# Latent-attention keys projected with features in rows, two heads per 128, and their turned part placed once for all heads

## The chip, the cores and the metric

One core of one Trainium2 chip runs the whole program. The metric is the device time of one execution in microseconds. The engines work side by side, each through its own instructions in an order fixed when the kernel is built: TensorE (PE in the profile; PEld is its weight load), VectorE (DVE), ScalarE (ACT), GpSimd (POOL); SyncE (SP) issues the transfers.

## The reference

A trunk of two layers over 256 positions of width 1024, in float32. In each layer one input projection feeds three causal token mixers (A: differential attention, 4 heads; B: dilated windows, 4 heads; C: latent attention, 8 heads); their gated sum and a gated feed-forward part follow. The change concerns mixer C:

```python
q = (_rms_norm(c_q, q_norm) @ w_uq).reshape(B, S, C_HEADS, C_NOPE_DIM + C_ROPE_DIM)
q_nope, q_pe = q[..., :C_NOPE_DIM], _rope(q[..., C_NOPE_DIM:], pos)
c_kv, k_pe = c_kv_pe[..., :C_KV_LORA], c_kv_pe[..., C_KV_LORA:]
k_pe = _rope(k_pe[:, :, None, :], pos)[:, :, 0]
kv = (_rms_norm(c_kv, kv_norm) @ w_ukv).reshape(B, S, C_HEADS, C_NOPE_DIM + C_V_DIM)
k_nope, v = kv[..., :C_NOPE_DIM], kv[..., C_NOPE_DIM:]
# scores: q_nope . k_nope + q_pe . k_pe, scale, causal softmax, times v
```

A head's key has 64 features of its own (k_nope, from w_ukv) and 32 that are turned by position (k_pe) and are the same for all 8 heads.

## The kernel before, in words

Every product is made of three matmuls: an operand x is split into a high part (ACT copies it, `hi_of`, line 223) and the residue (DVE subtracts, `lo_of`, lines 228 and 230), and high x high, high x low and low x high are summed in PSUM (`mm3`). The weights come in 294 pieces of up to 1024 columns: SP loads a piece, ACT and DVE split it three pieces ahead of its use (`split_piece`, `take`), and there are five buffers of each kind.

`dense` is a generator that goes through a layer's projections piece by piece; `pump(n)` advances it by n pieces, and `run` writes the smaller work between the pumps: the latent rows (`latent_scaled`, `latent_factors`, `latent_transposed`), in layer 0 also the bias tables on POOL (`tables`, lines 338 to 343), and then `attention`, which steps through 4 units of A, 8 of C and 4 of B, with one pump per step. That is the program's order. The order on each engine is made from it by a planner when the kernel is built (`schedule_with_timeline_sim=True`, line 1147): it simulates the engines and puts next on each what it reckons ready.

PSUM has 8 banks: 4 for the projections (`banks`, a ring) and 4 for attention and transposes (`att`). A bank is used again when the reads of its former content are done.

Latent attention before the change. `latent_scaled` copies the latent rows out of PSUM (cks: 256 key and value features and the 32 to be turned; tokens in partitions) and sums their squares. `latent_factors` makes the norm factors rq and rk (epsilon on DVE, the power on POOL, line 372), turns the 32 features on POOL (`rope`, lines 602 to 605, in the tile kpe) and copies them into k_tm for 8 heads (line 684). `latent_transposed` puts the features into partitions, with the norm's gains (line 693). `mla_up` projects: with the latent columns as the loaded operand and 512 weight columns moving it gets keys and values with tokens in partitions, in four banks (lines 573 to 580):

```python
for lhs, ww, s, e in ((h, wh, k == 0, False), (h, wl, False, False), (lo, wh, False, k == 1)):
    for f in range(2):
        self.mm(pu[b][f], lhs, ww[:, f * 512:f * 512 + 512], s, e)
```

The key half is copied with the factor rk into k_tm (line 588), the value half split with it into vc. Scores need features in partitions, so `head_pair`, called two steps ahead for each of four pairs of heads, transposes q_tm and k_tm on PE: two heads by two token blocks, four transposes for the queries and four for the keys (line 719), and splits both. `scores` then multiplies with 96 features in partitions. Behind the up projection comes the value projection of A (`v_proj`), which takes the next two of the four banks.

Of the kernel before, what the change touches and what calls it, by code (L numbers as in the profile page):

```python
# [12 lines left out]
F32 = mybir.dt.float32  # L13
# [7 lines left out]
DEPTH = 2  # L21
# [28 lines left out]
def weight_plan():  # L50
# [11 lines left out]
    for l in range(DEPTH):  # L62
# [3 lines left out]
        block("mla_w_ukv", l, 2, 0, 1024)  # L66
# [117 lines left out]
class Build:  # L184
# [104 lines left out]
    def setup(self):  # L289
# [29 lines left out]
        self.k_tm = cp.tile([128, 2, 8, 96], F32, name="k_tm")  # L319
# [4 lines left out]
        self.kpe = cp.tile([128, 2, 32], F32, name="kpe")  # L324
# [223 lines left out]
    def mla_up(self):  # L548
# [24 lines left out]
        pu = [[self.banks.get() for _ in range(2)] for _ in range(2)]  # L573
        for k in range(2):
            (wh, wl), = self.take()
            for b in range(2):
                h, lo = (t[:, k * 256 + b * 128:k * 256 + b * 128 + 128] for t in self.ck)
                for lhs, ww, s, e in ((h, wh, k == 0, False), (h, wl, False, False), (lo, wh, False, k == 1)):
                    for f in range(2):
                        self.mm(pu[b][f], lhs, ww[:, f * 512:f * 512 + 512], s, e)  # L580
            if k < 1:
                yield
        self.fr.put(*self.ck)
        for b in range(2):
            for f in range(2):
                kv = pu[b][f].rearrange("p (h d) -> p h d", h=4)
                s = self.rk[:, b:b + 1]
                nc.scalar.activation(out=self.k_tm[:, b, 4 * f:4 * f + 4, 0:64], in_=kv[:, :, 0:64], func=AF.Copy, scale=s)
                hi, lo = (self.vc[b][:, 4 * f:4 * f + 4, i] for i in range(2))
                self.split(hi, lo, kv[:, :, 64:128], s)  # L590
                self.banks.put(pu[b][f])
# [76 lines left out]
    def latent_factors(self, l):  # L668
        nc = self.nc
        nc.vector.tensor_scalar(out=self.vq, in0=self.vq, scalar1=EPS, scalar2=None, op0=ALU.add)  # L670
        nc.vector.tensor_scalar(out=self.vk, in0=self.vk, scalar1=EPS, scalar2=None, op0=ALU.add)
        self.rq = self.cp.tile([128, 2], F32, name=f"rq{l}")
        self.rk = self.cp.tile([128, 2], F32, name=f"rk{l}")
        rq = self.small()
        self.rsqrt(rq, self.vq)
        self.rsqrt(self.rk, self.vk)
        nc.vector.tensor_scalar(out=self.rq, in0=rq, scalar1=-(96 ** -0.5), scalar2=None, op0=ALU.mult)
        for b in range(2):
            t1, t2 = self.f.get(), self.f.get()
            kp = self.kpe[:, b]  # L680
# [113 lines left out]
    def unit_stages(self, kind, l, h):  # L794
# [93 lines left out]
        def scores():  # L888
# [3 lines left out]
            if c == 1:  # L892
                self.fr.put(*q)
                self.fr.put(k)
# [257 lines left out]
```

## Time and profile before

| | us |
|---|---|
| median of 3 runs | 883.79 (883.66 to 884.83) |
| profiled execution | 883.18 |
| its span | 881.4 |
| PE busy | 873.6 (99%) |
| weight loads of PE | 759.5 (86%) |
| DVE busy | 591.1 (67%) |
| ACT busy | 502.2 (57%) |
| POOL busy | 71.4 (8%) |

Times are those of one execution, counted from the span's start; layer 0 lies ahead of about 430 us, layer 1 behind. Matmuls are pipelined: they overlap in the records, so the distance between starts, not the mean duration, says what one costs on a full PE. A group such as "L719 PE MATMUL att<-ident,k_tm" is line 719, engine, operation, and the tiles written and read.

### The profile page before, as it was taken

Reading aid. Unit: us, or ns where it says so; the run is one execution under the profiler, and the core shown is the slowest. Engines: PE = TensorE matmul, PEld = TensorE weight load, DVE = VectorE, ACT = ScalarE, POOL = GpSimd, SP = SyncE. Lnnn points to the kernel's source line nnn. Section 1 sums busy time; section 2 is a strip of 40 time slices with the busy share of each in tenths; the row PEclk is TensorE's granted clock in tenths of the full one; section 3 lists DMA queues with packets and bytes.
Section 4 is the critical chain, followed back from the end, with each engine's and each line's share of the span. In section 5 each row is a group of like instructions: output and inputs, shape, how many; then the busy total and the mean of one; then the engine's idle time right before and its main releaser. Section 6 shows DMA issues by size and latency. Waiting matters only on the chain.

```text
span 881.4 us, 12736 instructions
## 1 busy us (share of the span) xinstructions
PE 873.6 (99%) x4710; PEld 759.5 (86%) x4710; DVE 591.1 (67%) x990; ACT 502.2 (57%) x852; POOL 71.4 (8%) x95
## 2 busy tenths in 40 slices
PE   9999999999999999999999999999999999999997
PEld 9989988888888888888899899888888888888886
DVE  5988878665666655555467888786556666656444
ACT  7797777644454444444376867775454644444332
POOL 1940310000000000000011303100000000000000
PEclk9999999999999999999999999999999999999999
DMA  9756444456656665656475553444555556655541
GB/s 340 245 170 209 128 141 160 146 169 193 187 167 197 187 190 182 182 186 191 127 226 174 172 168 128 151 145 159 180 189 182 167 193 202 203 190 180 181 141 49
DMA packets 45423, 155.92 MB, mean 177 GB/s; under 512 B 5168, under 2 KB 6192, under 8 KB 45360
## 3 DMA queue, kind: packets, MB, share of 16 engines
q1 hardware_dynamic: 44928, 154.55, 55.0%
q8 instruction: 37, 0.61, 0.3%
q10 hardware_dynamic: 432, 0.55, 0.2%
q14 instruction: 26, 0.21, 0.1%
HBM read 154.03 MB, written 1.05 MB: 176 GB/s over the span
## 4 chain that ended last, share of the span: by engine, by line
PE 97%; POOL 1%; issue 1%; DVE 0%; ACT 0%; POOLq 0%
PE bank L210 87%; PE att L210 6%; PE att L445 2%; PE att L719 1%; PE att L767 0%; PE att L768 0%; PE att L769 0%; POOL f L602 0%; PE att L693 0%; PE att L851 0%; POOL f L604 0%; POOL f L603 0%; POOL q_tm L605 0%; DVE x_tm L1043 0%; ACT x_tm L1058 0%
## 5 line engine op out<-in xcount | busy, mean ns | idle before, releaser
L210 PE MATMUL bank<-whi,fr 128*128 128x512 f32 (+1 forms) x2032 | 631.1, 387 | 0.0
L228 DVE TENSOR_TENSOR wlo<-raw,whi 128x1024 fp32r<-128x1024 f32 (+2 forms) x294 | 353.9, 1206 | 250.8 <-ACT whi L223 250.1
L223 ACT ACTIVATE whi<-raw 128x1024 fp32r<-128x1024 f32 (+2 forms) x294 | 305.0, 1041 | 305.8 <-PE bank L210 246.0
L210 PEld LDWEIGHTS bank<-whi,fr 128*128 128x128 f32 x2032 | 379.8, 188 | 71.5 <-ACT whi L223 0.2
L210 PE MATMUL bank<-wlo,fr 128*128 128x512 f32 (+1 forms) x1016 | 390.1, 386 | 0.0
L210 PEld LDWEIGHTS bank<-wlo,fr 128*128 128x128 f32 x1016 | 191.0, 188 | 35.5 <-DVE wlo L228 0.3
L210 PE MATMUL bank<-fr,whi 128*128 128x256 f32 x512 | 94.6, 285 | 0.0
L210 PEld LDWEIGHTS bank<-fr,whi 128*128 128x128 f32 x512 | 80.0, 192 | 0.2
L210 PE MATMUL bank<-fr,wlo 128*128 128x256 f32 x256 | 73.0, 285 | 0.0
L210 PEld LDWEIGHTS bank<-fr,wlo 128*128 128x128 f32 x256 | 49.0, 192 | 0.0
L372 POOL TENSOR_TENSOR r<-small,mhalf 128x2 f32<-128x2 f32 x4 | 2.8, 708 | 477.5 <-DVE small L398 462.6
L759 ACT ACTIVATE s<-s,small 128x256 f32<-128x256 f32 (+1 forms) x80 | 35.8, 455 | 1.2 <-DVE small L757 0.8
L372 POOL TENSOR_TENSOR small<-small,mhalf 128x2 f32<-128x2 f32 (+1 forms) x12 | 10.0, 831 | 280.5 <-DVE small L1047 178.5
L223 ACT ACTIVATE fr<-att 128x512 fp32r<-128x512 f32 (+2 forms) x54 | 28.3, 559 | 4.1 <-PE att L719 2.3
L210 PE MATMUL att<-whi,fr 128*128 128x288 f32 (+1 forms) x108 | 29.9, 290 | 0.0
L228 DVE TENSOR_TENSOR fr<-att,fr 128x512 fp32r<-128x512 f32 (+2 forms) x46 | 28.2, 634 | 0.1
L223 ACT ACTIVATE fr<-f 64x512 fp32r<-64x512 f32 (+2 forms) x40 | 23.3, 583 | 6.7 <-DVE f L516 5.4
L210 PE MATMUL att<-fr,fr 96*128 96x256 f32 (+3 forms) x152 | 26.0, 277 | 0.0
L210 PEld LDWEIGHTS att<-fr,fr 96*128 96x128 f32 (+1 forms) x152 | 22.7, 190 | 0.6
L615 ACT ACTIVATE f<-bank,rh 128x512 f32<-128x512 f32 x24 | 16.3, 689 | 11.7 <-PE bank L210 11.7
L972 ACT ACTIVATE f<-bank,rh 128x512 f32<-128x512 f32 (+1 forms) x24 | 15.6, 654 | 12.2 <-PE bank L210 12.2
L210 PEld LDWEIGHTS att<-whi,fr 128*128 128x128 f32 x108 | 20.4, 191 | 0.1
(134 smaller groups left out, 636.0 us busy)
## 6 DMA issues: line engine op xcount, KB each, us to landing
raw<-w SPq DMA_DIRECT2D x272, 512.0 KB, 3.6
raw<-w SPq DMA_DIRECT2D x16, 336.0 KB, 3.2
raw<-w SPq DMA_DIRECT2D x6, 384.0 KB, 3.6
x_tm<-xt SPq DMA_DIRECT2D x2, 512.0 KB, 6.4
f<-x SPq DMA_DIRECT2D x3, 256.0 KB, 5.2
f<-fnorm SPq DMA_DIRECT2D x2, 256.0 KB, 4.2
out<-x_tm ACTq DMA_DIRECT2D x2, 256.0 KB, 2.2
f<-x SPq DMA_DIRECT2D x2, 128.0 KB, 3.1
```

The costliest lines, as they stand in the source:

```text
L210: self.nc.tensor.matmul(out, lhsT, rhs, start=start, stop=stop, skip_group_check=True)
L223: self.nc.scalar.activation(out=hi, in_=src, func=AF.Copy, scale=scale)
L228: self.nc.vector.tensor_tensor(out=lo, in0=src, in1=h, op=ALU.subtract)
L372: self.nc.gpsimd.tensor_tensor(out=out, in0=v, in1=self.mhalf[:, 0:v.shape[1]], op=ALU.pow)
L445: self.nc.tensor.transpose(ps[:, c, b * 128:b * 128 + 128], src[b][:, c0 + c * 128:c0 + c * 128 + 128], self.ident)
L615: nc.scalar.activation(out=t[b], in_=bank[b], func=AF.Tanh, scale=self.rh[:, b:b + 1])
L719: nc.tensor.transpose(ps[0:96, c, b * 128:b * 128 + 128], src[:, b, 2 * p + c, :], self.ident)
L759: nc.scalar.activation(out=s[:, SL[b]], in_=s[:, SL[b]], func=AF.Exp, bias=mn[:, b:b + 1], scale=-1.0, accum_out=z[:, b:b + 1])
L972: nc.scalar.activation(out=a, in_=g, func=AF.Tanh, scale=self.rh[:, b:b + 1])
```

## The change

The columns of w_ukv are put in another order on the host (keys of all heads, then values of all heads). The keys are projected with the weights as the loaded operand and the 256 tokens moving, so that they come out with features in partitions, two heads per 128 rows. They are split from there into a new tile kc (keys of all heads, high and low), and k_tm and its transposes are gone. The values keep the old form. The factor rk now scales the latent rows ahead of their transposes, so latent_factors stands earlier in the program. The turned features stay on POOL in their own step (turned_keys); two transposes per layer and two splits with a broadcast over four heads (keys_placed) bring them into rows 64 to 96 of kc.

```diff
@@ -63,7 +63,7 @@
         block("w_in", l, KT, OFF_C, N_C)
         mixer_in(l, OFF_AQ)
         block("mla_w_uq", l, 3, 0, 768)
-        block("mla_w_ukv", l, 2, 0, 1024)
+        block("w_ukv", l, 2, 0, 1024)
         block("w_in", l, KT, OFF_AV, 512)
         mixer_in(l, OFF_BQ)
         block("w_in", l, KT, OFF_BV, 512)
@@ -316,12 +316,13 @@
         nc.sync.dma_start(out=self.ident, in_=self.cst_in[:, C_ID:C_ID + 128])
         self.vc = [cp.tile([128, 8, 2, 64], F32R, name=f"vc{b}") for b in range(2)]
         self.q_tm = cp.tile([128, 2, 8, 96], F32, name="q_tm")
-        self.k_tm = cp.tile([128, 2, 8, 96], F32, name="k_tm")
+        self.kc = cp.tile([128, 8, 2, 256], F32R, name="kc")
         self.low = [[cp.tile([128, 512], F32R, name=f"low{j}_{c}") for c in range(2)] for j in range(2)]
         for low in self.low:
             for c in range(2):
                 nc.gpsimd.memset(low[c][64 - c * 64:128 - c * 64].bitcast(F32), 0.0)
-        self.kpe = cp.tile([128, 2, 32], F32, name="kpe")
+        self.kpe = cp.tile([128, 2, 96], F32, name="kpe")
+        nc.gpsimd.memset(self.kpe, 0.0)
 
     def tables(self):
         nc, cp = self.nc, self.cp
@@ -570,25 +571,31 @@
             self.rope(qp, t1, t2, b, [128, 8])
             self.f.put(t1f, t2f)
         yield
-        pu = [[self.banks.get() for _ in range(2)] for _ in range(2)]
+        banks = [self.banks.get() for _ in range(4)]
+        pk, pv = banks[0:2], banks[2:4]
+        hi, lo = self.ck
         for k in range(2):
             (wh, wl), = self.take()
+            ts = slice(k * 256, k * 256 + 256)
+            for p in range(4):
+                s = slice(p * 128, p * 128 + 128)
+                self.mm3(pk[p // 2][:, (p % 2) * 256:(p % 2) * 256 + 256], wh[:, s], wl[:, s], hi[:, ts], lo[:, ts],
+                         k == 0 and p % 2 == 0, k == 1)
             for b in range(2):
-                h, lo = (t[:, k * 256 + b * 128:k * 256 + b * 128 + 128] for t in self.ck)
-                for lhs, ww, s, e in ((h, wh, k == 0, False), (h, wl, False, False), (lo, wh, False, k == 1)):
-                    for f in range(2):
-                        self.mm(pu[b][f], lhs, ww[:, f * 512:f * 512 + 512], s, e)
+                h, l = (t[:, k * 256 + b * 128:k * 256 + b * 128 + 128] for t in self.ck)
+                self.mm(pv[b], h, wh[:, 512:1024], k == 0, False)
+                self.mm(pv[b], h, wl[:, 512:1024], False, False)
+                self.mm(pv[b], l, wh[:, 512:1024], False, k == 1)
             if k < 1:
                 yield
         self.fr.put(*self.ck)
+        for p in range(4):
+            for c in range(2):
+                src = pk[p // 2][c * 64:c * 64 + 64, (p % 2) * 256:(p % 2) * 256 + 256]
+                self.split(self.kc[0:64, 2 * p + c, 0], self.kc[0:64, 2 * p + c, 1], src)
         for b in range(2):
-            for f in range(2):
-                kv = pu[b][f].rearrange("p (h d) -> p h d", h=4)
-                s = self.rk[:, b:b + 1]
-                nc.scalar.activation(out=self.k_tm[:, b, 4 * f:4 * f + 4, 0:64], in_=kv[:, :, 0:64], func=AF.Copy, scale=s)
-                hi, lo = (self.vc[b][:, 4 * f:4 * f + 4, i] for i in range(2))
-                self.split(hi, lo, kv[:, :, 64:128], s)
-                self.banks.put(pu[b][f])
+            self.split(self.vc[b][:, :, 0], self.vc[b][:, :, 1], pv[b].rearrange("p (h d) -> p h d", h=8))
+        self.banks.put(*banks)
         yield
 
     def rope(self, x, t1, t2, b, lead):
@@ -667,21 +674,35 @@
 
     def latent_factors(self, l):
         nc = self.nc
-        nc.vector.tensor_scalar(out=self.vq, in0=self.vq, scalar1=EPS, scalar2=None, op0=ALU.add)
-        nc.vector.tensor_scalar(out=self.vk, in0=self.vk, scalar1=EPS, scalar2=None, op0=ALU.add)
+        for v in (self.vq, self.vk):
+            nc.vector.tensor_scalar(out=v, in0=v, scalar1=EPS, scalar2=None, op0=ALU.add)
         self.rq = self.cp.tile([128, 2], F32, name=f"rq{l}")
-        self.rk = self.cp.tile([128, 2], F32, name=f"rk{l}")
-        rq = self.small()
+        rk, rq = self.small(), self.small()
+        self.rsqrt(rk, self.vk)
         self.rsqrt(rq, self.vq)
-        self.rsqrt(self.rk, self.vk)
+        for b in range(2):
+            nc.vector.tensor_scalar(out=self.cks[b][:, 0:256], in0=self.cks[b][:, 0:256], scalar1=rk[:, b:b + 1],
+                                    scalar2=None, op0=ALU.mult)
         nc.vector.tensor_scalar(out=self.rq, in0=rq, scalar1=-(96 ** -0.5), scalar2=None, op0=ALU.mult)
+
+    def turned_keys(self):
+        nc = self.nc
         for b in range(2):
             t1, t2 = self.f.get(), self.f.get()
-            kp = self.kpe[:, b]
+            kp = self.kpe[:, b, 64:96]
             nc.gpsimd.tensor_copy(kp, self.cks[b][:, 256:288])
             self.rope(kp, t1[:, 0:32], t2[:, 0:32], b, [128])
             self.f.put(t1, t2)
-            nc.gpsimd.tensor_copy(self.k_tm[:, b, :, 64:96], kp.unsqueeze(1).to_broadcast([128, 8, 32]))
+        self.f.put(*self.cks)
+
+    def keys_placed(self):
+        ps = self.att.get()
+        for b in range(2):
+            self.nc.tensor.transpose(ps[0:96, b * 128:b * 128 + 128], self.kpe[:, b], self.ident)
+        src = ps[64:96, 0:256].unsqueeze(1).to_broadcast([32, 4, 256])
+        for h in range(0, 8, 4):
+            self.split(self.kc[64:96, h:h + 4, 0], self.kc[64:96, h:h + 4, 1], src)
+        self.att.put(ps)
 
     def latent_transposed(self, l, which):
         nc = self.nc
@@ -706,25 +727,18 @@
             self.f.put(*self.cqs)
         else:
             self.ck = (hi, lo)
-            self.f.put(*self.cks)
 
     def head_pair(self, p):
         nc = self.nc
-        res = []
-        for src in (self.q_tm, self.k_tm):
-            bank = self.att.get()
-            ps = split_rows(bank)
-            for c in range(2):
-                for b in range(2):
-                    nc.tensor.transpose(ps[0:96, c, b * 128:b * 128 + 128], src[:, b, 2 * p + c, :], self.ident)
-            if src is self.k_tm:
-                res.append(self.key_pair(ps[0:96], slice(0, 96)))
-            else:
-                hi, lo = self.fr.get(), self.fr.get()
-                self.split(hi[0:96], lo[0:96], bank[0:96])
-                res.append((hi, lo))
-            self.att.put(bank)
-        return res
+        bank = self.att.get()
+        ps = split_rows(bank)
+        for c in range(2):
+            for b in range(2):
+                nc.tensor.transpose(ps[0:96, c, b * 128:b * 128 + 128], self.q_tm[:, b, 2 * p + c, :], self.ident)
+        hi, lo = self.fr.get(), self.fr.get()
+        self.split(hi[0:96], lo[0:96], bank[0:96])
+        self.att.put(bank)
+        return hi, lo
 
 
     def scores(self, q, k, table):
@@ -886,12 +900,11 @@
                 self.pairs[p] = self.head_pair(p)
 
         def scores():
-            q, k = self.pairs[p]
+            q = self.pairs[p]
             cs = slice(c * 256, c * 256 + 256)
-            u["s"] = self.scores((q[0][0:96, cs], q[1][0:96, cs]), k[0:96, c * 512:c * 512 + 512], self.tc_c)
+            u["s"] = self.scores((q[0][0:96, cs], q[1][0:96, cs]), self.kc[0:96, h].rearrange("p f t -> p (f t)"), self.tc_c)
             if c == 1:
                 self.fr.put(*q)
-                self.fr.put(k)
 
         def values():
             if h == 0:
@@ -1082,17 +1095,20 @@
             if l:
                 pump(2)
             self.latent_scaled()
+            pump(1)
+            self.latent_factors(l)
             if l == 0:
                 self.tables()
                 self.lambdas()
-            pump(1)
+            self.turned_keys()
             self.latent_transposed(l, 0)
             pump(1)
             self.latent_transposed(l, 1)
             pump(1)
             self.latent_transposed(l, 2)
-            self.latent_factors(l)
-            pump(14 if l else 13)
+            pump(1)
+            self.keys_placed()
+            pump(13 if l else 12)
             self.attention(l, pump)
             for _ in stream:
                 pass
@@ -1132,6 +1148,7 @@
     a = {k: np.asarray(v) for k, v in inputs.items()}
     gate, up = a["w_ffn_gate"], a["w_ffn_up"]
     a["w_ffn"] = np.concatenate([m[:, :, c:c + 512] for c in range(0, FF, 512) for m in (gate, up)], axis=2)
+    a["w_ukv"] = a["mla_w_ukv"].reshape(DEPTH, 256, 8, 2, 64).transpose(0, 1, 3, 2, 4).reshape(DEPTH, 256, 1024)
     w = pack_weights(a)
     gains = pack_gains(a["attn_norm"], a["ffn_norm"], a["diff_norm"], a["mla_q_norm"], a["mla_kv_norm"])
     assert gains.shape == (128, G_W)
@@ -1141,7 +1158,7 @@
               "xt": np.ascontiguousarray(a["x"].reshape(2, 128, D)), "w": w, "gains": gains, "lam": lam, "fnorm": fnorm,
               "cst": shape_constants()}
 
-    nc = bacc.Bacc("TRN2", target_bir_lowering=False, num_devices=1)
+    nc = bacc.Bacc("TRN2", target_bir_lowering=False, num_devices=1, dynamic_dma_scratch_size=1024)
     t = {k: nc.dram_tensor(k, v.shape, F32, kind="ExternalInput").ap() for k, v in arrays.items()}
     out = nc.dram_tensor("out", (S, D), F32, kind="ExternalOutput").ap()
     with tile.TileContext(nc, schedule_with_timeline_sim=True) as tc, ExitStack() as ctx:
```

## Rows read from the trace of the kernel before

**Rows 1.** The page: span, busy time and share of each engine, instructions.
```profile
span 881.4 us, 12736 instructions
PE 873.6 (99%) x4710; PEld 759.5 (86%) x4710; DVE 591.1 (67%) x990; ACT 502.2 (57%) x852; POOL 71.4 (8%) x95
```
**Rows 2.** The page: chain that ended last, share of the span by engine.
```profile
PE 97%; POOL 1%; issue 1%; DVE 0%; ACT 0%; POOLq 0%
```
**Rows 3.** Waits of PE, whole run: total us, times, longest us.
```profile
PE bank L210 <- DVE ones L304: 1.0, 1, 1.0
PE att L719 <- POOL q_tm L605: 0.5, 1, 0.5
```
**Rows 4.** The chain in order of time: start us, us, engine, tile, line, count.
```profile
78.25 2.88 PE bank L210 x24
...
102.93 0.87 PE att L719 x8
...
740.25 21.78 PE bank L210 x96
```
**Rows 5.** ACT in order of time, last square in layers 0 and 1: start, us, instruction.
```profile
29.90 0.25 ACT L663 ACTIVATION_READ_ACCUMULATOR f<-f 128x1 f32 x1
...
461.76 0.20 ACT L663 ACTIVATION_READ_ACCUMULATOR f<-f 128x1 f32 x1
```
**Rows 6.** POOL in order of time, layer 0: start, us, instruction, count.
```profile
24.23 4.49 POOL L338 TENSOR_SCALAR ta<-f 128x256 f32<-128x256 f32 x4
...
29.06 5.47 POOL L342 TENSOR_SCALAR tb<-f 128x256 f32<-128x256 f32 x4
...
38.99 1.14 POOL L372 TENSOR_TENSOR rk<-small,mhalf 128x2 f32<-128x2 f32 x1
...
44.07 0.46 POOL L605 TENSOR_TENSOR kpe<-f,f 128x32 f32<-128x32 f32 x2
...
52.86 0.75 POOL L602 TENSOR_TENSOR f<-q_tm,cs 128x256 f32<-128x256 f32 x1 [6.92 <-ACT q_tm L563]
...
53.99 1.44 POOL L604 TENSOR_TENSOR f<-q_tm,cs 128x128 f32<-128x128 f32 x1
...
59.30 0.45 POOL L604 TENSOR_TENSOR f<-q_tm,cs 128x128 f32<-128x128 f32 x1
```
**Rows 7.** DVE groups by form: count, busy us, mean ns, idle before.
```profile
L780 DVE TENSOR_SCALAR s<-s,small 128x256 f32<-128x256 f32 x24 | 8.5, 353 | 0.5
...
L911 DVE TENSOR_TENSOR f<-att,f 64x256 f32<-64x256 f32 x16 | 6.7, 418 | 4.7 <-ACT f L910 4.5
...
L230 DVE SCALAR_TENSOR_TENSOR vc<-bank,rk,vc 128x256 fp32r<-128x256 f32 x8 | 3.6, 473 | 0.0
```
**Rows 8.** DVE in order of time, layer 0: a weight split, idle before it.
```profile
53.76 1.35 DVE L228 TENSOR_TENSOR wlo<-raw,whi 128x1024 fp32r<-128x1024 f32 x1 [1.77 <-ACT whi L223]
```
**Rows 9.** PE in order of time: key transposes of both layers, end of up projection.
```profile
24.92 0.71 PE L693 MATMUL att<-ident,f 128*128 128x128 f32 x5
...
58.47 0.62 PE L210 MATMUL bank<-whi,fr 128*128 128x512 f32 x2
...
60.62 0.54 PE L719 MATMUL att<-ident,q_tm 128*96 128x128 f32 x3 [0.55 <-POOL q_tm L605]
...
61.01 0.47 PE L210 MATMUL bank<-whi,fr 128*128 128x512 f32 x1
...
465.59 0.60 PE L693 MATMUL att<-ident,f 128*128 128x128 f32 x4
```
**Rows 10.** ACT groups by form: count, busy us, mean ns, idle before.
```profile
L910 ACT ACTIVATE f<-att 64x256 f32<-64x256 f32 x16 | 6.1, 379 | 5.8 <-PE att L210 5.5
...
L223 ACT ACTIVATE vc<-bank,rk 128x256 fp32r<-128x256 f32 x8 | 3.9, 493 | 0.0
L588 ACT ACTIVATE k_tm<-bank,rk 128x256 f32<-128x256 f32 x8 | 3.9, 485 | 0.0
```
**Rows 11.** Windows: busy us (count) of PE, PEld, DVE, ACT, POOL; clock, DMA.
```profile
30.00:40.00 10.00, 10.00 (x86) 10.00 (x85) 9.88 (x16) 8.01 (x13) 9.84 (x8) 1.00 0.64 211
```

## The prediction

> **What bounds the kernel now.** I read the page's busy shares first, then the chain of work that ended last, then TensorE's own waits, and only then single stretches. The reader is to see in the first that PE works 873.6 of 881.4 us while DVE and ACT work 591 and 502 [rows 1]; in the second that the chain is 97% PE, so that time on it is saved only by taking columns from PE or holes from its queue [rows 2]; in the third that the holes are few: in 4710 matmuls PE waited twice, 1.0 us at the start and 0.5 us in layer 0 for the turned queries of line 605 [rows 3]. So a PE instruction that goes is worth its full pitch, and an engine beside it counts only where it makes PE wait. The pitches come from the chain in order of time, where pieces of one kind stand unmixed [rows 4]: 24 matmuls of 256 columns in 2.88 us, 0.120 us each; 96 of 512 columns in 21.78 us, 0.227 us each; eight transposes of line 719 in 0.87 us, 0.109 us each. The mean durations of the groups (272 ns for such a transpose) overlap and are not the price.
>
> **Part by part, on PE.** Line 719 loses the key half: 4 pairs x 4 transposes x 2 layers = 32, 32 x 0.109 = 3.49 us. keys_placed adds 2 transposes per layer of the same shape (128 rows by 96, moving 128 columns): 4 x 0.109 = 0.44 us. The up projection had 24 matmuls of 512 columns per layer. It keeps 12 of them for the values, and the other 12 become 24 of 256 columns with the weights as the loaded side, as the query and key projection already runs them in the 24-matmul piece: 2 layers x (24 x 0.120 - 12 x 0.227) = 2 x 0.156 = 0.31 us more. Scores read keys of the same shape and rows from another tile: nothing. Sum on PE: -3.49 + 0.44 + 0.31 = -2.74 us.
>
> **What moves on the other engines, and what hides it.** Four places can make PE wait.
>
> First, the factor of the keys. Before, it was applied after the up projection; now it scales the latent rows ahead of their transposes, so those transposes hang on a chain that they did not have: last square on ACT, epsilon on DVE, power on POOL, two scalings on DVE. In layer 0 the last square ends at 30.1 us [rows 5], the power took 1.14 us once it was its turn [rows 6], a 128x256 scaling by a column takes 0.35 us [rows 7], each of the two DVE steps can stand behind one weight split of 1.35 us [rows 8], and the power behind one table operation of 1.4 us (5.47 / 4, [rows 6]): 30.1 + 1.35 + 1.4 + 1.1 + 1.35 + 0.7 = 36.0 us. The transposes of the keys stood at 24.9 us [rows 9]. At that place PE would wait 11 us; anywhere after 36 us it waits for nothing, and the up projection that needs them begins only after 50 us. In layer 1 the square ends at 462.0 us [rows 5] and the transposes stood at 465.6 us [rows 9]: the chain takes 1.1 + 0.7 us without queues and 2.7 us more behind two weight splits, 4.5 us against 3.6, so PE would wait at most 0.9 us. The order of each engine is fixed when the kernel is built, by a planner that puts an instruction where it reckons its inputs ready, and the one wait that it left in 873 us was 0.5 us long [rows 3]. So I take 0 and keep 0 to 11 us for the range.
>
> Second, the turned keys. The same POOL operations (copy, lines 602 to 605) run as before, less four broadcast copies; but their end now releases two transposes on PE, where it used to release nothing before 60 us. In layer 0 they ended at 44.5 us behind the twelve operations of the tables [rows 6]. Behind the two transposes everything on PE is queued, the query and key projections first. Again the price is 0 where the planner's estimate holds.
>
> By the Trainium skill, SBUF — State Buffer, section "SBUF: two separate sides", a DVE instruction with two SBUF inputs and a GpSimd instruction that reads SBUF exclude one another for a whole instruction. The trace agrees: line 604 took 1.44 us beside the DVE split that ran from 53.76 us, and 0.45 us later on [rows 6, 8]. The rule speaks against the change: POOL's steps, which PE now waits for, can each come a DVE split later. If the planner left that out, the time is rival C's 887.1 us; if it counted it in, it is the forecast's.
>
> Third, the banks. The value projection behind the up projection takes the first two of four banks. Before, such a bank was freed by two ACT and one DVE operation of 0.49 and 0.47 us per 256 columns [rows 7, 10]; now each of the two key banks is freed by four splits of 64x256, 0.38 us on ACT and 0.42 us on DVE [rows 7, 10]. Eight in a row on DVE, after a first ACT step: 8 x 0.42 + 0.38 = 3.74 us. But the key matmuls now come first: the first bank is complete 6 x 0.120 + 6 x 0.227 = 2.08 us before the up projection ends, so the second bank is free 1.66 us after that end. It is wanted three matmuls, 0.68 us, after the value projection starts, and that started 61.01 - 58.92 = 2.09 us after the end (the last two matmuls begin at 58.47 us), with a-head scores and query transposes between [rows 9]. 2.09 + 0.68 against 1.66: covered with 1.1 us to spare. Without that cover the wait is 1.66 - 0.68 = 1.0 us per layer.
>
> Fourth, DVE's load in layer 0, where it was busy 9.88 of 10 us [rows 11]. Added there are two scalings (0.7 us) and two residues of 32x1024, for which the nearest row is a split of 1024 columns, 1.35 us [rows 8]; a bound from below is the 64x256 row, 0.42 us. That is 1.5 to 3.4 us. DVE stood idle 1.77 us before 53.76 us [rows 8], which takes up half of the larger figure. The larger work of the attention's key splits goes away. I take 0 for PE and keep 1.6 us.
>
> The clearing of kpe falls in POOL's idle start, and no transfer runs on POOL's queue, so the smaller scratch costs nothing that a row shows. The 0.5 us wait for line 605 may stay, go, or double: -0.5 to +0.5.
>
> **The sum.** The profiled execution took 883.18 us, span 881.4 and 1.8 around it. 883.18 - 2.74 = 880.4 us. The median of the runs shown is 883.79 us, 0.6 above the profiled one, so on that scale I forecast 881.0 us, 0.31% faster. Its own range, with half a microsecond for line 605 on either side and up to 0.9 us of wait in layer 1, is 880.5 to 882.4.
>
> **The rivals.** A: banks or DVE take it back. If ACT and DVE are more than 1.1 us behind at the end of the up projection (both are near full there), PE waits 1.0 us per layer, or, by the fourth point, 1.6 us in layer 0; -2.74 + 1.6 to 2.0 gives 882.7 to 883.1. For it: the saturated stretch. Against: the key banks are finished first, and layer 1 has room.
>
> B: the transposes were free. If they lay in holes of PE, taking them away moves nothing, and the 0.31 + 0.44 us added give 884.5. Against: PE's waits sum to 1.5 us.
>
> C, on the other side: in layer 0 PE stands at the keys' transposes or at keys_placed because POOL is later than the planner reckoned. It decides there alone and from a lateness of 2.7 us on. Its price: one POOL line took 0.45 or 1.44 us [rows 6]; eight table operations took 4.49 + 5.47 = 9.96 us, where one of that size took 0.75 us at its best [rows 6]. If the planner reckoned with the best, POOL comes 9.96 - 6.0 = 4.0 us late on these, and at the same rate, 0.5 us each, 2.0 more on the other four. A wait of 6.0 - 2.74 leaves +3.3: 887.1 us. For it: POOL was 98% busy there [rows 11], and no PE instruction of that stretch hung on it before. Against: in both layers the query transposes hung on POOL too, beside the same DVE splits, and waited 0.5 us in all.
>
> **How the numbers follow.** A measurement of this kernel can tell about 0.2%, 1.8 us: faster is below 882.0, slower above 885.6. Forecast 0.68 (0.65 of it below 882.0), A 0.16 (0.01 faster where it costs half, the rest within), B 0.03 (within), C 0.13, of which lateness up to 4.5 us ends within and more ends slower, 0.10 by its price. So faster 0.66, same 0.24, slower 0.10. The range 879.9 to 884.6 leaves out most of C and little else.
>
> **What would show it.** Right: line 719 with 32 transposes instead of 64 and four new ones at 0.11 us; 48 matmuls of 256 columns in place of 24 of 512; PE still above 99%, its waits under 2 us. Wrong: a PE wait on kpe, on the scaled rows or on the split of a key bank in the list of waits; idle PE near 25 to 45 us or 58 to 62 us of layer 0; or a stretch far from the change, such as the feed-forward part, that is longer.

## The result and the profile after

The changed kernel takes 895.87 us (median of 4 runs, 894.91 to 896.65), the kernel before 883.88 beside it: ratio 1.0134, interval 1.0119 to 1.0149. It is 12.0 us slower, where 2.9 us faster was forecast, and lies outside the range (879.9 to 884.6). The profiled execution took 896.56 us, its span is 894.8.

First the page after: instructions, busy time, the granted clock in 40 slices, the chain by engine, in answer to [rows 1, 2].

```profile
span 894.8 us, 12722 instructions
PE 878.8 (98%) x4706; PEld 762.6 (85%) x4706; DVE 599.6 (67%) x1002; ACT 505.4 (56%) x852; POOL 65.6 (7%) x92
PEclk9998999999999999999999899999999999999999
PE 90%; DVE 4%; POOL 2%; DMA 2%; issue 1%; ACT 0%; SPq 0%; POOLq 0%; ACTq 0%; DVEq 0%
```

PE still has 98% of the span, but the chain no longer is all PE: 4% is DVE. Two of the 40 slices show a lower clock, one in each layer. PE's waits, in answer to [rows 3] (waiting tile and line, awaited one, us in all, times, longest):

```profile
PE bank L210 <- DVE wlo L228: 1.8, 2, 1.6
PE att L701 <- POOL kpe L612: 1.7, 1, 1.7
PE att L737 <- DVE small L771: 1.5, 1, 1.5
PE att L210 <- DVE small L771: 1.5, 2, 1.1
PE bank L210 <- DVE ones L304: 1.0, 1, 1.0
PE att L737 <- POOL q_tm L612: 1.0, 1, 1.0
PE att L781 <- DVE small L771: 0.7, 2, 0.5
PE bank L210 <- ACT whi L223: 0.5, 1, 0.5
```

9.7 us in place of 1.5. The name of the new key tile, kc, isn't among them, so the list alone accuses the wrong work. Where the holes lie is seen in the windows (busy time and count of PE, PEld, DVE, ACT, POOL, then the granted clock), first of after, then of before:

```profile
60.00:70.00 10.00, 5.98 (x36) 4.93 (x35) 10.00 (x27) 9.90 (x34) 3.87 (x4) 0.85 0.61 172
70.00:80.00 10.00, 9.91 (x53) 9.17 (x54) 9.81 (x38) 6.56 (x20) 0.00 (x0) 0.81 0.30 104
500.00:510.00 10.00, 7.57 (x42) 6.00 (x41) 9.84 (x32) 9.23 (x27) 1.79 (x2) 0.86 0.48 158
510.00:520.00 10.00, 10.00 (x52) 9.13 (x52) 8.68 (x35) 5.29 (x17) 0.00 (x0) 0.80 0.35 107
```

```profile
60.00:70.00 10.00, 9.45 (x45) 7.85 (x45) 9.93 (x33) 9.43 (x26) 0.56 (x1) 1.00 0.57 177
500.00:510.00 10.00, 10.00 (x60) 8.91 (x59) 7.88 (x13) 6.29 (x9) 0.00 (x0) 1.00 0.65 211
```

Both layers lose time at the same place, behind the up projection. There the key splits ran as follows in layer 0, first on ACT (high parts), then on DVE (residues); start, length, in square brackets the idle time before.

```profile
62.41 0.65 ACT L223 ACTIVATE kc<-bank 64x256 fp32r<-64x256 f32 x2
...
66.81 0.38 ACT L223 ACTIVATE kc<-bank 64x256 fp32r<-64x256 f32 x1
...
71.83 0.38 ACT L223 ACTIVATE kc<-bank 64x256 fp32r<-64x256 f32 x1 [0.93 <-DVE kc L228]
73.53 0.71 ACT L223 ACTIVATE kc<-bank 64x256 fp32r<-64x256 f32 x2 [1.33 <-DVE kc L228]
```

```profile
64.40 0.41 DVE L228 TENSOR_TENSOR kc<-bank,kc 64x256 fp32r<-64x256 f32 x1
...
70.07 0.42 DVE L228 TENSOR_TENSOR kc<-bank,kc 64x256 fp32r<-64x256 f32 x1
...
74.55 0.77 DVE L228 TENSOR_TENSOR kc<-bank,kc 64x256 fp32r<-64x256 f32 x2
```

A high part waits for a residue, though nothing that it reads is written by it; ACT's list of waits (both layers) has this three times:

```profile
ACT kc L223 <- DVE kc L228: 3.4, 3, 1.3
```

The eight splits take from 62.41 to 75.32 us. Until then their two banks are held, and the value projection of A, which began at 61.01 us [rows 9], begins at 75.66. PE fills the time with what the planner put there, and stands before it: the query transposes, the heads of A, one piece of weights.

```profile
44.29 0.31 PE L701 MATMUL att<-ident,kpe 128*96 128x128 f32 x1 [1.70 <-POOL kpe L612]
...
56.52 0.40 PE L210 MATMUL bank<-fr,whi 128*128 128x256 f32 x2
...
56.88 0.40 PE L210 MATMUL bank<-fr,whi 128*128 128x256 f32 x2
...
64.00 0.53 PE L737 MATMUL att<-ident,q_tm 128*96 128x128 f32 x3 [0.97 <-POOL q_tm L612]
...
66.01 0.39 PE L210 MATMUL att<-fr,fr 128*128 128x256 f32 x1 [1.06 <-DVE small L771]
...
70.09 0.58 PE L210 MATMUL bank<-fr,wlo 128*128 128x256 f32 x1 [1.60 <-DVE wlo L228]
70.47 0.63 PE L210 MATMUL bank<-fr,whi 128*128 128x256 f32 x2
...
71.11 0.63 PE L210 MATMUL bank<-fr,whi 128*128 128x256 f32 x2
...
75.66 0.47 PE L210 MATMUL bank<-whi,fr 128*128 128x512 f32 x1
```

At 56.5 us three matmuls of 256 columns take 56.88 - 56.52 = 0.36 us, at 70.5 us 0.64 us. The granted clock says why (the same stretch in steps of 2 us):

```profile
63.00:65.00 2.00, 0.98 (x8) 0.80 (x7) 2.00 (x10) 2.00 (x6) 0.87 (x2) 1.00 0.87 223
65.00:67.00 2.00, 0.67 (x4) 0.53 (x4) 2.00 (x10) 1.97 (x5) 0.00 (x0) 0.99 0.71 285
67.00:69.00 2.00, 1.33 (x5) 1.04 (x5) 2.00 (x6) 1.95 (x8) 0.00 (x0) 0.50 0.01 2
69.00:71.00 2.00, 0.91 (x4) 0.91 (x5) 1.94 (x4) 1.83 (x7) 0.00 (x0) 0.50 0.85 236
71.00:73.00 2.00, 2.00 (x11) 2.00 (x11) 1.94 (x7) 0.38 (x1) 0.00 (x0) 0.50 0.62 176
73.00:75.00 2.00, 2.00 (x17) 2.00 (x16) 1.97 (x10) 1.47 (x5) 0.00 (x0) 0.81 0.28 113
```

PE was busy 0.98 and 0.67 of two stretches of 2 us; then the clock stood at 0.50 (1.2 GHz), and it came back to 1.0 (2.4 GHz) in 73 to 75 us, after PE had been busy all of 71 to 73. So here the holes are paid twice, as holes and as slow matmuls behind them. The clock stood at 0.50 in one such stretch per layer, and else only in the last 1.8 us of the span, where PE does nothing, as in the last 1.8 us of before:

```profile
66.95:73.78 6.83, 5.02 (x22) 4.73 (x23) 6.70 (x18) 4.45 (x15) 0.00 (x0) 0.50 0.50 151
507.27:514.10 6.83, 6.36 (x29) 5.77 (x29) 6.74 (x23) 3.37 (x12) 0.00 (x0) 0.50 0.26 79
```

Two terms then make the account. PE's waits beyond the 1.5 us of before are 9.7 - 1.5 = 8.2 us. The clock cost at most half of the time that PE was busy at 0.50, (5.02 + 6.36) / 2 = 5.7 us (an estimate; by the pitches of 0.36 and 0.64 us it is 5.0). With the forecast's -2.74 that makes 11.2 us, where the span grew by 13.4: 2.2 us of the growth have no name.

### The profile page after: what moved, and what is told of

The parts are those of the page before. It is cut to its first block, busy times and chain, and to the rows that moved or that the text cites. A ratio compares the mean times of both kernels' runs of the same rounds, so it can differ in the third digit from the quotient of the medians.

```text
span 894.8 us, 12722 instructions
## 1 busy us (share of the span) xinstructions
PE 878.8 (98%) x4706; PEld 762.6 (85%) x4706; DVE 599.6 (67%) x1002; ACT 505.4 (56%) x852; POOL 65.6 (7%) x92
## 4 chain that ended last, share of the span: by engine, by line
PE 90%; DVE 4%; POOL 2%; DMA 2%; issue 1%; ACT 0%; SPq 0%; POOLq 0%; ACTq 0%; DVEq 0%
PE bank L210 81%; PE att L210 5%; PE att L446 2%; DVE wlo L228 2%; DMA f<-cst 1%; DMA raw<-w 1%; DMA x_tm<-xt 1%; DVE s L771 1%; POOL tb L343 1%; POOL ta L339 1%; POOL tb L344 0%; POOL small L373 0%; PE att L781 0%; PE att L783 0%; PE att L782 0%
## 5 line engine op out<-in xcount | busy, mean ns | idle before, releaser
L210 PE MATMUL bank<-whi,fr 128*128 128x512 f32 (+2 forms) x2016 | 628.1, 387 | 0.5 <-ACT whi L223 0.5
L210 PE MATMUL bank<-wlo,fr 128*128 128x512 f32 (+2 forms) x1008 | 387.5, 386 | 0.0
L210 PE MATMUL bank<-fr,whi 128*128 128x256 f32 x544 | 104.8, 292 | 0.0
L210 PEld LDWEIGHTS bank<-fr,whi 128*128 128x128 f32 x544 | 88.1, 198 | 0.5
L210 PE MATMUL bank<-fr,wlo 128*128 128x256 f32 x272 | 79.5, 293 | 1.8 <-DVE wlo L228 1.8
L210 PEld LDWEIGHTS bank<-fr,wlo 128*128 128x128 f32 x272 | 53.8, 198 | 2.6 <-DVE wlo L228 2.5
L223 ACT ACTIVATE fr<-att 128x512 fp32r<-128x512 f32 (+2 forms) x46 | 24.0, 552 | 3.2 <-PE att L737 1.5
L228 DVE TENSOR_TENSOR fr<-att,fr 128x512 fp32r<-128x512 f32 (+2 forms) x38 | 23.0, 627 | 0.6 <-ACT fr L223 0.6
L622 ACT ACTIVATE f<-bank,rh 128x512 f32<-128x512 f32 x24 | 16.4, 688 | 11.2 <-PE bank L210 11.0
L986 DVE SCALAR_TENSOR_TENSOR f<-f,bank 128x512 f32<-128x512 f32 (+1 forms) x24 | 15.4, 644 | 4.9 <-ACT f L985 4.9
L223 ACT ACTIVATE pt<-att 128x384 fp32r<-128x384 f32 x32 | 15.6, 486 | 4.2 <-PE att L783 3.6
```

The lines of the kernel that those rows point to most:

```text
L210: self.nc.tensor.matmul(out, lhsT, rhs, start=start, stop=stop, skip_group_check=True)
L223: self.nc.scalar.activation(out=hi, in_=src, func=AF.Copy, scale=scale)
L228: self.nc.vector.tensor_tensor(out=lo, in0=src, in1=h, op=ALU.subtract)
L622: nc.scalar.activation(out=t[b], in_=bank[b], func=AF.Tanh, scale=self.rh[:, b:b + 1])
L986: nc.vector.scalar_tensor_tensor(out=a, in0=a, scalar=1.0, in1=g, op0=ALU.add, op1=ALU.mult)
```

## The experiments

What each of ACT's highs waits for is recorded in the trace beside the instruction. Of the eight highs of layer 0 in the changed kernel the first two wait for the semaphore that PE raises, the six others for the one that DVE alone raises (its residues raise it). In layer 1 it is two and six again.

The program splits a bank in turn: high of one head, its residue, high of the next. Reads of one bank by two engines are ordered one behind the other in the built program, so "in turn" becomes a chain that goes back and forth between two engines that are both busy with other work. That the bank orders them, and not the tile kc that all of them write, is seen in his_first (below): there ACT makes the highs of the second bank before DVE has begun a residue of the first, and none of the eight waits for DVE. By the Trainium skill, "PSUM — Partial Sum Buffer", section "PSUM bank collisions raise a hardware error", two engines must not touch the same bank in the same 32 partitions at once, reads included, and it is for the program to order them. The trace agrees that they are ordered (3.4 us in three waits of ACT). The page lets different 32-partition groups of a bank be read together, and the two heads of a pair do lie in different ones; here they were ordered all the same (by halves of a bank four of the eight highs would wait for DVE, not six), and no run tried to part them.

My theory was this chain; the rivals were the placed transposes early in PE's order, the banks that the value projection waits for whatever the order of the splits, and the mere work that was added to ACT and DVE. In all tables the ratio is to the kernel before (883.78 to 883.92 us beside each), "waits" is the sum of PE's list, "clock" the mean granted clock of the profiled execution.

### All highs of a bank before its residues

The cuts from the edits, here and below, are shortened; lines with # are remarks.

```diff
-            for c in range(2):
-                self.split(self.kc[0:64, 2 * p + c, 0], self.kc[0:64, 2 * p + c, 1], src)
 # parts: the four heads of one bank
+            for h, src in parts:
+                self.hi_of(self.kc[0:64, h, 0], src)
+            for h, src in parts:
+                self.lo_of(self.kc[0:64, h, 1], src, self.kc[0:64, h, 0])
```

The same in keys_placed. his_first does this to the changed kernel. The control takes the kernel before, whose value split of a bank was one ACT and one DVE operation for four heads, and cuts it into four per bank: before_in_turn in turn, before_his_first with highs first; these two do the same operations. vbk_in_turn puts the turn back into the best version below.

> The changed kernel (895.9 us) with one order changed: per PSUM bank all high parts on ACT first, then all residues on DVE, for the key banks and for the placed turned part; the operations and their sizes are the same. Theory chain: reads of one bank by ACT and DVE are put one behind the other, so splitting in turn makes a chain of eight links per key bank that frees the banks late; with four highs first the chain has two links, the holes of PE after the up projection go, the clock stays at 1.0, and the time is 882 to 885 us. Rival load: DVE is simply too full after the up projection (the same operations run); the time stays at 893 to 897. Rival POOL: the wait on the turned keys (1.7 us) starts the trouble; the time stays above 890.

> The kernel before (883.9 us) with one thing done: each value half of a bank is split head by head in turn (ACT, DVE, ACT, DVE ...), four heads per bank, where it was one ACT and one DVE operation. Nothing else of the change. Theory chain: banks are freed late, PE gets holes and a clock under 1.0 near 60 to 80 us and in the same place of layer 1; 889 us or more. Rival load: 24 more small operations on ACT and on DVE, spread over two layers, slow it as much as before_his_first does, under 3 us; the two come out alike.

> Control to before_in_turn: the same 128x64 operations in the kernel before, but four highs of a bank on ACT first and then four residues on DVE. Theory chain: 883 to 886 us, clock 0.999. Rival load: as slow as before_in_turn, whatever that is.

> values_before_keys (882.0 us) with the splits of the key banks and of the placed part in turn again (ACT, DVE, ACT, DVE). Only the order of these operations differs. If the chain costs only where a projection waits for the key banks: 882 to 884 us, for the next projection takes the value banks. If it costs by itself, by breaking up ACT's and DVE's queues: 886 us or more.

| | median us (range, runs) | ratio (interval) | waits | clock |
|---|---|---|---|---|
| after | 895.87 (894.91 to 896.65, 4) | 1.0134 (1.0119 to 1.0149) | 9.7 | 0.991 |
| his_first | 889.73 (889.48 to 890.74, 4) | 1.0070 (1.0055 to 1.0085) | 7.3 | 0.996 |
| before_in_turn | 902.70 (901.42 to 903.33, 4) | 1.0213 (1.0198 to 1.0228) | 10.1 | 0.986 |
| before_his_first | 883.86 (883.01 to 884.99, 10) | 1.0001 (0.9991 to 1.0010) | 2.3 | 0.998 |
| vbk_in_turn | 885.37 (884.64 to 886.77, 10) | 1.0016 (1.0007 to 1.0025) | 4.7 | 0.999 |

The control settles that the turn costs by itself: the same operations cost 0.0 us with highs first and 18.8 us in turn, in a kernel that has nothing else of the change. It isn't the number of operations. But his_first, at 889.73, missed the 882 to 885 us of the theory: in the changed kernel the turn is about half of the loss. In his_first the eight highs of layer 0 are one run on ACT and the eight residues one run on DVE:

```profile
63.58 3.13 ACT L223 ACTIVATE kc<-bank 64x256 fp32r<-64x256 f32 x8
```

```profile
66.81 3.48 DVE L228 TENSOR_TENSOR kc<-bank,kc 64x256 fp32r<-64x256 f32 x8
```

6.7 us in place of 12.9, and PE is released at 68.6 in place of 75.7 us:

```profile
68.58 0.80 PE L210 MATMUL bank<-whi,fr 128*128 128x512 f32 x1 [1.75 <-DVE kc L228]
```

6.1 of the 12.0 us are gone, the rest isn't; now kc itself stands in PE's list (2.4 us in two waits). In the best version the turn costs 3.4 us (881.95 to 885.37), between the two ranges that were expected: the eight splits of layer 0 take from 60.38 to 81.79 us there, and PE's list has 3.0 us of waits for kc again, but the clock stays at 1.00 wherever PE works. In before_in_turn PE was busy 10.67 us in the stretch at 0.50 of layer 0 (63.42 to 77.07) and 7.95 us in that of layer 1 (510.56 to 520.80), so the clock cost up to 9.3 us beside 10.1 - 1.5 = 8.6 us of waits.

```profile
60.00:70.00 10.00, 6.37 (x32) 4.59 (x32) 9.96 (x46) 9.98 (x37) 1.35 (x3) 0.67 0.51 158
70.00:80.00 10.00, 9.09 (x33) 7.47 (x33) 7.28 (x37) 5.01 (x20) 0.00 (x0) 0.65 0.12 48
```

### Where the turned keys are placed

no_placing leaves out keys_placed, so the turned part of the keys is zero. hf_late is his_first with keys_placed moved to the first step of latent attention; vbk_early moves it back in the best version.

```diff
 # head preparation of latent attention
+            if h == 0:
+                self.keys_placed()
 # ahead of the up projection
-            self.keys_placed()
```

> The changed kernel without keys_placed: the turned rows of the keys are zeros, written once at the start (the scores lack the turned part). It takes away PE's wait for POOL (1.7 us in layer 0) and 2.4 us of DVE and 2.0 us of ACT per layer ahead of the up projection, and leaves the splits of the key banks in turn. Theory chain: the holes behind the up projection stay, 890 to 894 us. Rivals load and POOL: most of the 12 us goes, under 886.

> his_first (889.7 us) with keys_placed moved from ahead of the up projection to the attention, two steps before the first head that reads the keys. Rival load (what is left of the loss is the 2.4 us of DVE and 2.0 us of ACT per layer that now stand ahead of the saturated stretch, and PE's 1.7 us wait for POOL in layer 0): 883 to 886 us. If what is left is the key banks alone: 887 to 889 us.

> values_before_keys (882.0 us) with keys_placed back ahead of the up projection. If the early placing costs by itself (PE waits 1.7 us for the turned keys in layer 0; 2.4 us of DVE and 2.0 us of ACT per layer stand ahead of the saturated stretch): 884 to 887 us, with the wait on kpe in the list. If it costs only together with the wait for the key banks: under 883 us.

| | median us (range, runs) | ratio (interval) | waits | clock |
|---|---|---|---|---|
| no_placing | 893.13 (891.76 to 893.89, 4) | 1.0105 (1.0090 to 1.0120) | 8.6 | 0.993 |
| hf_late | 886.30 (885.75 to 887.85, 7) | 1.0032 (1.0021 to 1.0043) | 4.3 | 0.996 |
| vbk_early | 884.63 (884.29 to 885.47, 10) | 1.0010 (1.0000 to 1.0019) | 4.3 | 0.998 |

Leaving it out takes 2.7 us from after. Moving it late gives 3.4 us (his_first to hf_late), moving it back costs 2.7 (values_before_keys, below, to vbk_early). In vbk_early the waits that come back are the first place's own and that of the queries behind it:

```profile
PE att L708 <- POOL kpe L619: 1.7, 1, 1.7
PE att L746 <- POOL q_tm L619: 1.2, 1, 1.2
```

So the early transposes are a second cause, and a smaller one. (hf_late, at 886.30, lies between the ranges of its two cases, and no_placing and vbk_early came out as their first cases say.) hf_late has one wait left that is worth a name:

```profile
PE bank L210 <- DVE kc L228: 3.0, 1, 3.0
```

### The values first

The value projection takes the first two of four banks, and these were the keys'. values_first (on the changed kernel) and hf_values (on his_first) only split the values first and give their banks back first. values_before_keys (on hf_late) takes both weight pieces, runs all value matmuls first, splits the values, and only then the keys:

```diff
-        pk, pv = banks[0:2], banks[2:4]
+        pv, pk = banks[0:2], banks[2:4]
 # per piece: value matmuls only; behind both pieces:
+        # split both value banks
+        for p in range(4):
+            for k in range(2):
+                self.mm3(key columns of p, piece k)
 # split the key banks, highs first
-        self.banks.put(*banks)
+        self.banks.put(*pv, *pk)
```

> The changed kernel (895.9 us) with the splits in turn as they are, but the value banks split first and given back first, so that the next projection takes them and not the key banks. Theory chain, in the form that PE starves because the value projection waits for the key banks: 884 to 889 us. If it stays at 893 or more, the chain costs by keeping ACT and DVE from their other work, not by that one projection.

> his_first (889.7 us) with the value banks split and given back first. If what is left of the loss is the value projection's wait for eight key splits (1.8 us of PE wait in layer 0 and the clock after it): 885 to 887 us. If it is load: unchanged, 889 to 890 us.

> hf_late (886.3 us) with the up projection in another order: all value matmuls first, into the two banks that come free first, their splits, and then all key matmuls; the next projection takes the value banks. So the eight key splits of a layer are made beside that projection and not ahead of it. If what is left of the loss is PE waiting for key banks (3.0 us in layer 0) and the clock that falls behind that wait: 881 to 883 us, waits of PE under 2 us and the clock at 0.999. If ACT and DVE are too full whatever the order: 885 us or more.

| | median us (range, runs) | ratio (interval) | waits | clock |
|---|---|---|---|---|
| values_first | 890.64 (889.97 to 891.53, 4) | 1.0078 (1.0063 to 1.0093) | 6.5 | 0.994 |
| hf_values | 896.58 (895.97 to 898.61, 4) | 1.0148 (1.0133 to 1.0163) | 10.0 | 0.991 |
| values_before_keys | 881.95 (881.23 to 883.33, 11) | 0.9982 (0.9973 to 0.9991) | 2.5 | 0.999 |

values_before_keys takes 4.4 us from hf_late and is 1.8 us faster than the kernel before (883.78 beside it; 0.8 to 2.4 us by the interval). The key splits still are late (the last ends at 71.1 us), but nothing on PE waits for them (its waits sum to 2.5 us, where under 2 was expected):

```profile
PE bank L210 <- DVE ones L304: 1.0, 1, 1.0
PE bank L210 <- ACT whi L223: 0.8, 2, 0.5
PE bank L210 <- DVE vc L228: 0.4, 1, 0.4
PE bank L210 <- ACT q_tm L564: 0.3, 1, 0.3
```

```profile
60.00:70.00 10.00, 9.58 (x48) 8.01 (x47) 9.91 (x32) 9.91 (x30) 1.86 (x2) 1.00 0.41 134
```

DVE and ACT are as full as in after; PE isn't in their way. hf_values was a miss: the banks that it gives back first are those that the matmuls complete last, so PE waits for the value splits:

```profile
PE bank L210 <- DVE vc L228: 3.6, 2, 2.1
```

The order of return alone cost 6.9 us on his_first and was worth 5.2 us on the changed kernel (values_first, 890.64, between its two ranges); together with the order of the matmuls, and on hf_late, it came with a gain of 4.4. Why the two signs differ I can't settle: the planner orders every engine anew for each program, and two edits aren't a sum of their parts.

### Fewer splits, and the factor alone

Four splits of 64x512 (two heads of a bank at once) in place of eight of 64x256: on hf_late (hf_four_late), on it with values_first's order of splits (four_values_late), and on the best version (vbk_four).

```diff
-                self.hi_of(self.kc[0:64, h, 0], src)
+                self.hi_of(self.kc[0:64, h:h + 3:2, 0], src)
```

> All together: highs first, four key splits of 64x512 per layer instead of eight of 64x256, value banks first, keys placed in the attention. If chain, banks and load are the whole loss, PE's waits fall to 2 us, the clock stays at 0.999, and the forecast of the document comes back: 881 to 882.5 us, faster than before. If something else holds PE: above 884 us.

> hf_late (886.3 us) with four key splits of 64x512 per layer instead of eight of 64x256. By the durations of before (ACT 0.63 against 2 x 0.38, DVE 0.70 against 2 x 0.42 us) this takes 0.5 us per layer from each engine ahead of the wait for the key banks. If the amount of work decides: 885 to 886 us. If the planner's placing decides: anything from 883 to 890, without a relation to the 0.5 us.

> values_before_keys (882.0 us) with four key splits of 64x512 per layer instead of eight of 64x256. PE's waits on banks were 0.7 us there, so less work for ACT and DVE should give nothing: 881.5 to 882.3 us. If the saturated stretch still holds PE through other waits: 881 us or less.

before_prescaled takes the kernel before and does only the first step of the change: the factor of the keys scales the latent rows, with latent_factors earlier; keys keep their form and their transposes.

```diff
-                nc.scalar.activation(out=self.k_tm[:, b, 4 * f:4 * f + 4, 0:64], in_=kv[:, :, 0:64], func=AF.Copy, scale=s)
+                nc.scalar.activation(out=self.k_tm[:, b, 4 * f:4 * f + 4, 0:64], in_=kv[:, :, 0:64], func=AF.Copy)
 # latent_factors, now ahead of the transposes
+            nc.vector.tensor_scalar(out=self.cks[b][:, 0:256], in0=self.cks[b][:, 0:256], scalar1=rk[:, b:b + 1],
+                                    scalar2=None, op0=ALU.mult)
```

> The kernel before (883.9 us) with one part of the change done: the key factor scales the latent rows ahead of their transposes, latent_factors ahead of the tables, the turning behind them; keys still in k_tm, transposed per pair. Forecast of the document: no cost, 883.5 to 885 us. Rival POOL: PE stands at the transposes of the scaled rows in layer 0, 885 us or more with that wait in the list.

| | median us (range, runs) | ratio (interval) | waits | clock |
|---|---|---|---|---|
| four_values_late | 892.36 (891.98 to 893.27, 4) | 1.0100 (1.0083 to 1.0117) | 7.7 | 0.994 |
| hf_four_late | 883.33 (882.96 to 884.16, 10) | 0.9996 (0.9987 to 1.0005) | 3.1 | 0.999 |
| vbk_four | 882.48 (882.28 to 883.53, 11) | 0.9986 (0.9977 to 0.9995) | 2.0 | 0.998 |
| before_prescaled | 884.49 (884.19 to 884.80, 10) | 1.0009 (1.0000 to 1.0018) | 2.0 | 0.999 |

Where PE waits for the key banks, half as many splits give 3.0 us (hf_late to hf_four_late): the wait for kc falls from 3.0 to 1.4 us, and the clock stays at 1.00, where PE was busy 3.41 us at 0.50 in hf_late. That is more than the 0.5 us of work per layer, and by the expectation the planner's placing. Where PE doesn't wait for them, it gives nothing (values_before_keys to vbk_four, the intervals overlap). four_values_late is a second miss, and its trace names one cause: the placed transposes themselves, which in hf_late began at 71.4 us without a wait, end their wait at 64.6, where they want a bank of attention that DVE hasn't read out yet:

```profile
64.58 0.63 PE L703 MATMUL att<-ident,kpe 128*96 128x128 f32 x2 [3.95 <-DVE small L775]
```

Moved late they hang on the attention's banks instead of on POOL. Why the planner put them there in this program and later in the others stays open. The factor alone costs 0.8 us by its ratio, and nothing at the lower end of the interval, as expected.

## Why the prediction was wrong

The account from the result, for the runs whose causes are told above, in us against the profiled execution of before. "Clock" is half of the time that PE was busy at a clock of 0.50, an estimate from above; "rest" is what the three terms leave of the longer span.

| | PE sum | waits | clock | together | span - 881.4 | rest |
|---|---|---|---|---|---|---|
| after | -2.74 | +8.2 | +5.7 | +11.2 | +13.4 | 2.2 |
| his_first | -2.74 | +5.8 | +1.5 | +4.6 | +6.3 | 1.7 |
| hf_late | -2.74 | +2.8 | +1.7 | +1.8 | +3.1 | 1.3 |
| values_before_keys | -2.74 | +1.0 | 0.0 | -1.7 | -1.2 | 0.5 |
| before_in_turn | 0 | +8.6 | +9.3 | +17.9 | +20.1 | 2.2 |

**PE's sum held in direction, and in 1.2 to 2.2 of its 2.74 us.** The counts are the forecast's: 4 transposes of kpe, 32 of the queries, 544 in place of 512 matmuls of the group fr,whi with 256 columns, the form of the 24-matmul piece [rows 4]. What the sum is worth is seen best in the five changed kernels whose clock stayed at 1.00 wherever PE worked (values_before_keys, vbk_in_turn, vbk_early, vbk_four, hf_four_late): their spans less PE's waits are 877.7 to 878.7 us, where before has 879.9. That is -1.2 to -2.2 us, not -2.74; and before_prescaled, with PE's work unchanged, has 880.5, so 0.6 us of it can be the planner's order. The rest in the table is of the same kind, and before_in_turn, whose PE work is that of before, has it too; no run tells what it is. Where the splits don't stand in PE's way, the kernel comes to 881.95 us, not 884.5, and rival B falls with this.

**The third place, the banks, is the step that failed.** I reckoned "Eight in a row on DVE, after a first ACT step: 8 x 0.42 + 0.38 = 3.74 us". The durations were right:

```profile
L228 DVE TENSOR_TENSOR kc<-bank,kc 64x256 fp32r<-64x256 f32 x16 | 6.5, 415 | 0.2
L223 ACT ACTIVATE kc<-bank 64x256 fp32r<-64x256 f32 x16 | 5.9, 378 | 3.9 <-DVE kc L228 3.4
```

What was wrong is "in a row". It took for granted that ACT reads the next head while DVE reads this one. They share a bank; each handover puts the next operation behind whatever ACT or DVE, both busy 9.9 of 10 us or more from 60 to 70 us, have in their order, and 3.74 us became 12.9 (6.7 with the highs first: the durations in a row, but hardly side by side). The kernel before never showed this, since its splits were one operation of each engine per bank and kind. "Covered with 1.1 us to spare" then was 13.8 us between the end of the up projection, counted as in the forecast (the next matmul begins at 61.89 us), and the start of the value projection at 75.66, where 2.09 had been counted. The splits also began late: the last key matmul starts at 59.24 us, the first high at 62.41. Rival A had the place, the direction and this lateness, but took its price from the same sum: 1.0 us per layer. Step by step, 6.1 us (the turn), 3.4 (the early transposes) and 4.4 (the values first) lead from 895.87 to 881.95: 10.5 of the 13.9 us belong to this place, the clock that fell with them included.

**The second place** was priced at nothing because the planner's estimate would hold. It didn't: PE stood 1.70 us at the transposes of kpe, and with what follows it is worth 2.7 to 3.4 us. Rival C named this place and mechanism; its 6.0 us were too much, and it wasn't the main cause. That one POOL wait of 0.5 us had come out of the planner before was weak evidence for a new one.

**The first and the fourth place** held: PE waits nowhere for the scaled rows, and the first alone, in before_prescaled, costs 0.0 to 0.18%. The residue of 32x1024, bounded by 0.42 and 1.35 us, took 1.22.

**The clock was in no term.** Every rival priced a wait at its length. In after the holes brought up to 5.7 us of clock beside 8.2 of waits, in before_in_turn up to 9.3 beside 8.6. Not every hole did: in vbk_in_turn PE's list sums to 4.7 us and in vbk_early to 4.3, and the clock stayed at 1.00 wherever PE worked. The trace of before could have warned only by its 1.00 wherever PE works: a PE that hardly stops has never shown what stopping costs.

## What to carry to other kernels

Where two engines read one bank, write all reads of the one ahead of all reads of the other, and when a split is cut into smaller ones, ask again who orders the pieces: the cut cost nothing or 18.8 us by that alone. Give a ring's buffers back in the order in which they are completed, and run first the matmuls whose banks are wanted next (4.4 us here, in one pair of runs). Price a hole in a PE that is full at up to twice its length (8.2 us of waits brought up to 5.7 more, 8.6 up to 9.3, the 3.2 us that vbk_in_turn has beyond before none). Don't take one pair of programs for a proof where a planner orders each anew: the same return of banks gave 5.2 us in one and cost 6.9 in another, and what the argument rests on, the turn (18.8, 6.1 and 3.4 us) and the early transposes (2.7, 3.4 and 2.7), had the same sign in three pairs each. And look for the cause not in the list of PE's waits but in what holds the buffers that its queue needs.

## What was not expected of the hardware

The granted clock fell to 0.50 behind short holes of a kernel whose PE is 98% busy; in the whole kernel before it is 1.00 wherever PE works. Three holes of 0.97, 1.06 and 0.48 us, which ended at 64.00, 66.01 and 67.16 us of after, went with a clock at 1.2 GHz from 66.95 to 73.78 us, in which matmuls of 256 columns had a pitch of 0.21 in place of 0.12 us, though PE worked without a stop from 70.09 us on.
